# Statistics matmuls in four column tiles, the last score level in two halves of the array, a new order of the opening and five smaller edits in a hybrid RG-LRU / HGRN2 / SSD layer

## The chip, the cores and the metric

The kernel runs on one core of a Trainium2 chip. The metric is the device time of one execution in microseconds (us), the median of three runs. A profiled execution stands beside it: its trace gives the start and the length of each instruction on each engine. PE is the matrix engine (PEld its weight loads), DVE the vector engine, ACT the scalar engine, POOL the GpSimd engine, and SP the queue that issues most of the transfers from memory.

## The reference, cut to what matters

One decoder layer on 2048 tokens of width 1024; three mixers share one input projection (1024 to 5648 columns) and one output projection (2048 to 1024).

```python
h = rmsnorm(x, norm_w) * (1 + scale) + shift        # scale, shift = cond @ w_ada
u = h @ w_in                                        # split over the three mixers
ya = rg_lru(conv(a_x), ...) * silu(a_g)             # 512 wide
yb = rmsnorm(hgrn2_chunked(q, k, v, log_f), hg_norm_w) * silu(hg_g)   # 512 wide, 4 heads
yc = groupwise rmsnorm(ssd_chunked(...) * silu(ssd_z))                # 1024 wide, 2 groups
y = concat([ya, yb, yc]) @ w_out
out = rmsnorm(x + gate * y)
```

All matrix work is in float32. The projections split each operand into a rounded high and a low part (float32r) and run three passes, high by high, high by low and low by high; the small matmuls take plain float32 operands, and the trace shows two records for each of those.

## The kernel before, in words

The tokens are handled in four blocks of 512, two at a time: a first half (blocks 0 and 1) and a second half (blocks 2 and 3). Channels lie on the partitions, tokens along the free axis.

*The opening.* For the first two blocks the string `PROG` (line 41) writes out the order of the opening by hand, one token for each step. `X` loads a block of transposed x (eight transfers of 256 KB), `D` loads one of eight pieces of the modulation weights (four transfers of 256 KB, line 434), `w` and `W` load and split the first three projection weights, in two halves of the contraction. `S` squares x on ACT and sums the squares on DVE (`norm_sum`, line 299; seven additions), `Q` sums over the partitions on PE (line 311), `R` spreads the result over the partitions (line 320, evacuated by ACT). `A` is the modulation matmul of one piece (line 441, 16 records in the trace), whose result ACT copies to `macc`; `C` turns it into a column (line 450) that DVE finishes. `H` with block and piece makes one piece of h: DVE scales x (`h_pre`), ACT writes the high part (line 330), DVE the low part (line 332). `M` with block and piece are the nine matmuls of that piece for the forget, query and gate projections of head 0 (line 339). `U` is a number of warming matmuls on ones (line 1004). PE runs its instructions in exactly this order; a scheduler places those of the other engines. SP issues transfers in order and keeps eight of them under way.

*The rest of a half.* `weave` (line 382) spreads the serial work of a branch between the pieces of the next projections: a branch is a generator, each of its `yield`s has a weight, and after each the share of the pieces that is due is written. `pend` is the list of branches for the next stretch of projections.

- `hgrn` (line 553) is the gated recurrence of one head for both blocks: seven score levels (levels 0 to 5 in column tiles of 32, `ps_sA` and `ps_sB`; the last, `ps_sC`, line 609, with 64 weight columns), between them multiplications of Q and K on DVE and POOL; then transposes (`ps_kt`), the state products (`ps_kv`), and the output `ps_o` (lines 645 and 649), block after block in the single bank of the pool `ps_oy`.
- `stats` (line 521) sums the squares of a branch's outputs, `acc`, over the channels: four matmuls for a block, the weights 128 tokens of `acc`, the moving operand one column of ones. There are two for each of the three norms in each half.
- `ssd_bc`, `ssd_a`, `ssd_b` are the state space branch; its `ps_y` (lines 792 and 797) writes the two halves of the partitions in turn, 64 weight columns each. `lru` is the RG-LRU, whose activations are chained in order by `sact` (line 151).
- `norm_gen` (line 883) makes the norm of blocks 2 and 3 during the first half: square root on ACT, reciprocal on DVE (line 285), `ps_rb` on PE.

*The output projection.* `fetch` (line 913) reads a group's branch outputs back and splits them, the low part by default on POOL, and `unit` runs the matmuls `po` (line 1138).

## Time and profile before

| what | us |
|---|---|
| median of 3 runs (1697.58 to 1697.99) | 1697.59 |
| the profiled execution, its own time | 1699.3 |
| its span, from the first instruction to the last | 1697.5 |
| PE busy with matmuls | 1653.0 (97%) |
| DVE / ACT / POOL busy | 971.5 / 748.6 / 757.3 |

The times that follow are counted from the start of the span. A group of instructions carries its line, its engine, and output<-inputs by the names in the program; a bracket behind it gives the idle time of its engine just before and what ended that. Matmuls are pipelined: how long a block of them holds PE is read from its start to the start of the next block, not from the length of one.

### The profile page before, as it was taken

Reading aid. Unit: us, or ns where it says so; the run is one execution under the profiler, and the core shown is the slowest. Engines: PE = TensorE matmul, PEld = TensorE weight load, DVE = VectorE, ACT = ScalarE, POOL = GpSimd, SP = SyncE. Lnnn points to the kernel's source line nnn. Section 1 sums busy time; section 2 is a strip of 40 time slices with the busy share of each in tenths; the row PEclk is TensorE's granted clock in tenths of the full one; section 3 lists DMA queues with packets and bytes.
Section 4 is the critical chain, followed back from the end, with each engine's and each line's share of the span. In section 5 each row is a group of like instructions: output and inputs, shape, how many; then the busy total and the mean of one; then the engine's idle time right before and its main releaser. Section 6 shows DMA issues by size and latency. Waiting matters only on the chain.

```text
span 1697.5 us, 29336 instructions
## 1 busy us (share of the span) xinstructions
PE 1653.0 (97%) x11452; PEld 1349.2 (79%) x11452; DVE 971.5 (57%) x1726; ACT 748.6 (44%) x1640; POOL 757.3 (45%) x630
## 2 busy tenths in 40 slices
PE   8799999999999999899999999999999999999998
PEld 4688877888887877788887788888877777888886
DVE  5654766557645746646756555655568646444443
ACT  4422323366556656632322456554757623222221
POOL 1233344355635764345334346545756543222223
PEclk9899999999999999999999999999999999999999
DMA  9412010032425342231110032323334544333231
GB/s 333 116 26 63 27 39 26 26 113 82 116 71 155 88 125 76 62 89 45 29 55 27 27 100 75 94 56 106 88 103 133 171 120 150 97 96 99 89 93 61
DMA packets 177691, 150.60 MB, mean 89 GB/s; under 512 B 14545, under 2 KB 137937, under 8 KB 177553
## 3 DMA queue, kind: packets, MB, share of 16 engines
q1 hardware_dynamic: 141216, 123.82, 25.1%
q10 hardware_dynamic: 33936, 17.04, 3.4%
q0 software_dynamic: 2400, 7.87, 1.3%
q8 instruction: 90, 1.47, 0.4%
q14 instruction: 49, 0.39, 0.1%
HBM read 123.40 MB, written 25.30 MB: 88 GB/s over the span
## 4 chain that ended last, share of the span: by engine, by line
PE 85%; DVE 4%; DMA 3%; ACT 3%; issue 3%; POOL 2%; SPq 0%; POOLq 0%; ACTq 0%; DVEq 0%
PE po L1138 19%; PE ps_x L339 10%; PE ps_z L339 9%; PE ps_v L345 6%; PE ps_f L339 5%; PE ps_g L339 5%; PE ps_bc L339 5%; PE ps_q L339 4%; PE ps_lg L339 4%; PE ps_lx L339 4%; PE ps_y L792 2%; PE ps_bx L768 2%; PE ps_y L797 1%; PE ps_sA L565 1%; PE ps_o L645 1%
## 5 line engine op out<-in xcount | busy, mean ns | idle before, releaser
L1138 PE MATMUL po<-wo,yy 128*128 128x512 f32 x1512 | 353.3, 395 | 2.5 <-POOL yy L69 1.6
L1138 PEld LDWEIGHTS po<-wo,yy 128*128 128x128 f32 x1512 | 283.8, 188 | 71.5 <-POOL yy L69 2.4
L142 POOL TENSOR_TENSOR w<-raw,w 128x512 fp32r<-128x512 f32 x156 | 219.6, 1426 | 266.9 <-ACT w L141 223.4
L72 DVE SCALAR_TENSOR_TENSOR cacc<-craw,col,cacc 128x512 f32<-128x512 f32 x192 | 203.8, 1062 | 47.6 <-ACT cacc L66 36.3
L339 PE MATMUL ps_z<-ht,w 128*128 128x512 f32 x768 | 190.2, 399 | 0.8 <-ACT halo L66 0.8
L339 PE MATMUL ps_x<-ht,w 128*128 128x512 f32 x768 | 190.4, 400 | 0.0
L339 PEld LDWEIGHTS ps_z<-ht,w 128*128 128x128 f32 x768 | 141.9, 188 | 34.7 <-issue 2.1
L339 PEld LDWEIGHTS ps_x<-ht,w 128*128 128x128 f32 x768 | 141.1, 189 | 28.6
L72 DVE SCALAR_TENSOR_TENSOR o<-po,rstd,o 128x512 f32<-128x512 f32 x64 | 47.2, 749 | 119.4 <-PE po L1138 98.8
L69 POOL TENSOR_TENSOR yy<-yr,yy 128x512 fp32r<-128x512 f32 x61 | 78.7, 1310 | 80.7 <-ACT yy L66 73.4
L69 POOL TENSOR_TENSOR hg_k<-hg_k,hg_t 128x256 f32<-128x256 f32 x80 | 60.2, 770 | 120.6 <-PE ps_sA L565 61.3
L141 ACT ACTIVATE w<-raw 128x512 fp32r<-128x512 f32 x158 | 92.3, 627 | 42.0 <-issue 22.0
L339 PE MATMUL ps_f<-ht,w 128*128 128x512 f32 x384 | 99.5, 406 | 5.4 <-DVE ht L72 5.4
L339 PE MATMUL ps_bc<-ht,w 128*128 128x512 f32 x384 | 101.0, 406 | 0.0
L345 PE MATMUL ps_v<-vw,ht 128*128 128x264 f32 x768 | 98.8, 289 | 0.0
L339 PE MATMUL ps_q<-ht,w 128*128 128x512 f32 x384 | 98.7, 403 | 0.0
L339 PE MATMUL ps_lx<-ht,w 128*128 128x512 f32 x384 | 97.7, 408 | 0.0
L345 PEld LDWEIGHTS ps_v<-vw,ht 128*128 128x128 f32 x768 | 95.7, 191 | 1.2 <-DVE l_gs L69 0.2
L69 POOL TENSOR_TENSOR s_ce<-s_ce,cacc 128x512 f32<-128x512 f32 x64 | 93.5, 1481 | 1.5 <-ACT s_ce L66 1.5
L339 PE MATMUL ps_lg<-ht,w 128*128 128x512 f32 x384 | 93.2, 397 | 0.0
L339 PE MATMUL ps_g<-ht,w 128*128 128x512 f32 x336 | 92.0, 408 | 0.0
L339 PEld LDWEIGHTS ps_f<-ht,w 128*128 128x128 f32 x384 | 71.2, 191 | 23.4 <-DVE ht L72 5.7
(260 smaller groups left out, 2853.1 us busy)
## 6 DMA issues: line engine op xcount, KB each, us to landing
raw<-in_w_in SPq DMA_DIRECT2D x176, 256.0 KB, 3.2
s_cb<-crd SPq DMA_DIRECT2D x64, 256.0 KB, 3.8
yr<-yscr SPq DMA_DIRECT2D x64, 256.0 KB, 3.2
xr<-in_x SPq DMA_DIRECT2D x48, 256.0 KB, 3.4
xt<-in_x_t SPq DMA_DIRECT2D x32, 256.0 KB, 4.7
wta<-in_w_mod SPq DMA_DIRECT2D x32, 256.0 KB, 5.9
yscr<-cacc ACTq DMA_DIRECT2D x32, 256.0 KB, 2.7
rawo<-in_w_out SPq DMA_DIRECT2D x32, 256.0 KB, 3.9
```

Of the source, the lines that this page charges most:

```text
L69: e.tensor_tensor(o, a, b, op=op)
L72: V.scalar_tensor_tensor(o, a, s, b, op0=op0, op1=op1)
L141: after(S.activation(hi, raw, AF.Copy), None if eng is V else dep)
L142: after(eng.tensor_tensor(lo, raw, hi, op=SUB), dep if eng is V else None)
L339: d_ = PE.matmul(ps, b.hl[wl][:, k, :], ht[:, hl, :], start=(k == 0 and n == 0), stop=(k == KT - 1 and n == 2))
L345: d_ = PE.matmul(ps[:, 0:264], ht[:, hl, c * P:(c + 1) * P], b.vw[k // 4][wl][:, k % 4, :], start=(k == 0 and n == 0), stop=(k == KT - 1 a ...
L565: PE.matmul(out(n, c, r), Ks[n][:, o:o + 32], mv[n][..., o + sh:o + sh + 32], start=True, stop=True)
L645: PE.matmul(po[:, c], v[:, c], ssb[:, 4 * n + c], start=True, stop=ci == 0)
L768: PE.matmul(pkv[:, c].rearrange("p h n -> p (h n)"), bt[:, c], xw[:, c].rearrange("p h n -> p (h n)"), start=True, stop=True)
L792: PE.matmul(py[64 * hh:64 * hh + 64, c], xdt[:, c, hh], Ms[hh][:, c], start=True, stop=sv[tb][c] is None)
L797: PE.matmul(py[64 * hh:64 * hh + 64, c], sv[tb][c][:, 64 * hh:64 * hh + 64], Cs[hh][:, c * P:(c + 1) * P], start=False, stop=True)
L1138: PE.matmul(pss[t, n], yys[u, t][yl][:, k4, :], wts[4 * fam + k4][wl][n], start=(k4 == 0 and i == 0), stop=(k4 == 3 and i == 2))
```

## The change

1. `PROG` is written anew. The second block of x is loaded behind the third modulation piece instead of ahead of the eighth, its squares and its norm come before M03, and from then on the pieces of both blocks alternate. The squares of both blocks share four buffers of the weight pool, and the first x takes buffers of the pool for h. Two warming matmuls are added before M03. Each scaling (`h_pre`) is ordered behind the low part of the piece before the last.
2. The 32 row parameters (`rowp`) are loaded at the start by ACT's queue, and `aneg` is made from them there, not at the end of the first half's recurrences.
3. `stats` takes both blocks in one go; each group of 128 tokens becomes four matmuls with 32 weight columns, in four column tiles: 32 matmuls instead of 2 x 4.
4. The last score level puts the first block on partitions 0 to 63 and the second on 64 to 127, and alternates between them; two copies evacuate it.
5. `ps_o` of the second block takes a bank of `ps_sc`.
6. Each `hgrn` gets a gap of weight 2 ahead of it.
7. Square root and reciprocal of the norms of blocks 2 and 3 are made ahead of the second RG-LRU stretch, both at once.
8. The low part of units 4 and 5 of the output projection is made by DVE.

```diff
-PROG = ("X0 D0 w0 D1 D2 S0 U8 A0 Q0 U1 C0 D3 R0 W0 A1 U1 C1 H00 D4 A2 M00 C2 H01 w1 W1 D5 A3 M01 C3 H02 D6 A4 M02 C4 H03 X1 "
-        "A5 M03 C5 H04 D7 A6 M04 C6 H05 S1 M05 H06 Q1 A7 R1 M06 C7 H10 H07 B K M10 H11 M11 H12 M07 H13 M12 H14 M13 "
-        "H15 M14 H16 M15 H17 E M16 M17")
+PROG = ("X0 D0 w0 D1 D2 X1 S0 U8 A0 Q0 U1 C0 D3 R0 W0 A1 U1 C1 H00 H01 A2 M00 C2 w1 H02 M01 S1 M02 D4 A3 Q1 C3 R1 H03 "
+        "H10 U2 W1 M03 D5 A4 M10 H11 C4 M11 H12 H04 M12 H13 M13 D6 A5 M04 H14 C5 H05 M14 D7 A6 M05 H15 C6 H06 M15 A7 M06 H16 C7 "
+        "H07 B K M16 H17 E M07 M17")
...
-        after(nc.sync.dma_start(rowp, rows[0:1, 0:32].to_broadcast([P, 32])), dep)
...
     def early():
+        nc.scalar.dma_start(rowp, rows[0:1, 0:32].to_broadcast([P, 32]))
...
+        sact(aneg, rowp[:, 16:32], AF.Exp)
+        V.tensor_scalar(aneg, aneg, -1.0, None, op0=MUL)
...
-    def stats(acc, fam, tb):
+    def stats(accs, fam, tbs):
         yield
         pq = bank(ps_ms, "ms", "pq")
-        for i in range(4):
-            PE.matmul(pq[:, i:i + 1], acc[:, i * P:(i + 1) * P], ones[:, 0:1], start=True, stop=True)
-        act(ssq[:, fam, 4 * tb:4 * tb + 4], pq[:, 0:4], AF.Copy)
+        for n, tb in enumerate(tbs):
+            for i in range(4):
+                for r in range(4):
+                    o = i * P + 32 * r
+                    PE.matmul(pq[32 * r:32 * r + 32, 4 * n + i:4 * n + i + 1], accs[tb][:, o:o + 32], ones[:, 0:1],
+                              start=True, stop=True)
+        act(ssq[:, fam, 4 * tbs[0]:4 * tbs[0] + 8], pq[:, 0:8], AF.Copy)
         yield
...
+                for c in range(4):
+                    for n in range(2):
+                        o = c * P
+                        PE.matmul(pC[64 * n:64 * n + 64, c], Ks[n][:, o:o + 64], Qs[n][:, o + 64:o + P],
+                                  start=True, stop=True)
                 for n in range(2):
-                    for c in range(4):
-                        o = c * P
-                        PE.matmul(pC[0:64, 4 * n + c], Ks[n][:, o:o + 64], Qs[n][:, o + 64:o + P],
-                                  start=True, stop=True)
-                act(ssb[0:64, :, 64:P], pC[0:64], AF.Copy)
+                    act(ssb[0:64, 4 * n:4 * n + 4, 64:P], pC[64 * n:64 * n + 64, 0:4], AF.Copy)
...
-            po = bank(ps_oy, "oy", "ps_o", (P, 4, P))
+            pool, tag = ((ps_oy, "oy"), (ps_sc, "sc"))[n]
+            po = bank(pool, tag, "ps_o", (P, 4, P))
...
     def norm_gen(xs, st):
-        rb = norm_rows(rsqrt_cols(st))
+        rb = norm_rows(st)
...
-                sqs = [[hp.tile([P, 2, TB], F32, tag="h", name="xsq") for _ in range(4)] for _ in tbs]
-                x0s = [wp.tile([P, 2, TB], F32, tag="w", name="xt") for _ in range(4)]
+                x0s = [hp.tile([P, 2, TB], F32, tag="h", name="xt") for _ in range(4)]
+                sqs = [wp.tile([P, 2, TB], F32, tag="w", name="xsq") for _ in range(4)]
...
-            pend = [(hgrn(h, tbs, {tb: fq[h, tb] for tb in tbs}, {tb: vs[tb][0] for tb in tbs}, acc, h == 0), HGW)]
+            pend = [(gap(2), 2), (hgrn(h, tbs, {tb: fq[h, tb] for tb in tbs}, {tb: vs[tb][0] for tb in tbs}, acc, h == 0), HGW)]
...
-        if half == 0:
-            act(aneg, rowp[:, 16:32], AF.Exp)
-            V.tensor_scalar(aneg, aneg, -1.0, None, op0=MUL)
...
-        st_ = [(stats(acc[tb], 0, tb), 2) for tb in tbs]
+        st_ = [(stats(acc, 0, tbs), 2)]
...
-            late = [(stats(acc[tb], 1 + g, tb), 2) for tb in tbs]
+            late = [(stats(acc, 1 + g, tbs), 2)]
...
+            if i == 1 and half == 0:
+                xst = {n: rsqrt_cols(st) for n, st in xst.items()}
...
-            fetch(u + 1)
+            fetch(u + 1, V if u + 1 in (4, 5) else G)
```

Three places show where the instructions went.

ACT in the opening. `xt_210` and `xt_211` before, and `xt_205` and `xt_206` in the change, are buffers of the first block's x, `xt_255` to `xt_269` in the change the pieces of the second block's; `ht` is the high part of a piece of h. Before:

```order
L66 ACTIVATE rb_320<-ps_rb_315 128x512
L141 ACTIVATE wt_326<-raw_238 128x512
L330 ACTIVATE ht_350<-xt_210,gsc_83 128x512
L66 ACTIVATE macc_339<-psm_330 128x256
L330 ACTIVATE ht_388<-xt_210,gsc_83 128x512
L66 ACTIVATE macc_370<-psm_361 128x256
```

In the change:

```order
L66 ACTIVATE xsq_209<-xt_255 128x512
L330 ACTIVATE ht_365<-xt_205,gsc_83 128x512
L66 ACTIVATE xsq_209<-xt_257 128x512
L66 ACTIVATE macc_354<-psm_345 128x256
L66 ACTIVATE xsq_210<-xt_259 128x512
L66 ACTIVATE xsq_210<-xt_261 128x512
L66 ACTIVATE xsq_211<-xt_263 128x512
L66 ACTIVATE xsq_211<-xt_265 128x512
L66 ACTIVATE macc_381<-psm_372 128x256
L66 ACTIVATE xsq_212<-xt_267 128x512
L330 ACTIVATE ht_369<-xt_205,gsc_83 128x512
```

The squares of the second block now stand ahead of the first two pieces of h and of the copies of the second and third modulation results; before, they stood behind all but two of the first block's pieces.

PE at the end of the first half's third stretch of projections (`ps_bc`), around the statistics of the recurrence. Before:

```order
L649 MATMUL ps_o<-hg_q,hst_177 128x128
L339 MATMUL ps_bc<-ht,w 128x512 x3
L525 MATMUL pq<-ones,acc 128x1 x4
L339 MATMUL ps_bc<-ht,w 128x512 x6
L525 MATMUL pq<-ones,acc 128x1 x4
L669 MATMUL ps_bt<-ident,cacc 128x128 x4
```

In the change:

```order
L653 MATMUL ps_o<-ssb,hg_v 128x128
L657 MATMUL ps_o<-hg_q,hst_180 128x128
L339 MATMUL ps_bc<-ht,w 128x512 x6
L530 MATMUL pq<-ones,acc 32x1 x32
L677 MATMUL ps_bt<-ident,cacc 128x128 x4
```

The sums of the second block stood nine projection matmuls behind the last output, and now stand six behind it.

ACT around the square root of the norm of block 3 (`xst_5300` before, `xst_5347` in the change; `xst_5044` is that of block 2). Before, at the start of the second half:

```order
L152 ACTIVATE l_r_6806<-ps_r_6802,col_74 128x512
L152 ACTIVATE l_i_6808<-ps_i_6803,col_74 128x512
L152 ACT_TABLE_LOAD
L152 ACTIVATE xst_5300<-xst_5300,epsc_92 128x4
L141 ACTIVATE w_6734<-raw_6736 128x512
L141 ACTIVATE w_6734<-raw_6740 128x512
L66 ACTIVATE rb_6825<-ps_rb_6820 128x512
```

In the change, ahead of the activations of the first RG-LRU stretch:

```order
L152 ACTIVATE l_gs_6185<-ps_lg_6118 128x512
L152 ACT_TABLE_LOAD
L152 ACTIVATE xst_5044<-xst_5044,epsc_92 128x4
L152 ACTIVATE xst_5347<-xst_5347,epsc_92 128x4
L66 ACTIVATE s_z_5910<-cacc_5783 128x512
L520 DMA yscr1_100<-cacc_5783 128x4x128
L152 ACT_TABLE_LOAD
L152 ACTIVATE l_r_6206<-ps_r_6202,col_74 128x512
```

Both roots now come some eighty microseconds of PE work earlier, with one more table load on either side of them.

## Rows read from the trace of the kernel before

**Rows 1.** The page's first two parts: the span, and the busy time of each engine.

```profile
span 1697.5 us, 29336 instructions
...
PE 1653.0 (97%) x11452; PEld 1349.2 (79%) x11452; DVE 971.5 (57%) x1726; ACT 748.6 (44%) x1640; POOL 757.3 (45%) x630
```

**Rows 2.** Who waited for whom on PE, over the whole span: the line that waited, what it waited for, us in total, times, the longest.

```profile
PE ps_rb L320 <- DVE xst L285: 7.3, 2, 5.5
PE ps_f L339 <- DVE ht L72: 5.4, 1, 5.4
PE ps_ss L311 <- DVE xsq L305: 3.9, 1, 3.9
PE psm L450 <- ACT macc L66: 2.9, 1, 2.9
...
PE ps_o L645 <- DVE hg_g L69: 1.9, 2, 1.1
PE ps_sA L565 <- POOL hg_q L69: 1.8, 1, 1.8
PE po L1138 <- POOL yy L69: 1.6, 2, 0.9
```

**Rows 3.** PE in order of time, in the opening (start, length, instructions with their count, idle time before them in brackets).

```profile
21.40 1.86 PE L441 MATMUL psm<-wta,condz 128*32 128x256 f32 x16
...
37.37 0.50 PE L450 MATMUL psm<-ones,macc 128*128 128x1 f32 x4
37.80 1.07 PE L441 MATMUL psm<-wta,condz 128*32 128x256 f32 x16
...
71.18 0.86 PE L339 MATMUL ps_f<-ht,w 128*128 128x512 f32 x3
...
73.26 0.86 PE L339 MATMUL ps_f<-ht,w 128*128 128x512 f32 x3
...
85.10 0.86 PE L339 MATMUL ps_g<-ht,wt 128*128 128x512 f32 x3
...
88.36 0.65 PE L565 MATMUL ps_sA<-hg_q,hg_k 128*32 128x64 f32 x32 [1.82 <-POOL hg_q L69]
```

**Rows 4.** Windows of the opening and of the start of the second half: length, busy time of PE, PEld, DVE, ACT and POOL with counts, then PE's granted clock, the share of the transfer engines and GB/s.

```profile
65.00:70.00 5.00, 5.00 (x12) 3.91 (x13) 4.84 (x7) 4.17 (x7) 2.58 (x2) 0.51 0.03 10
693.00:698.00 5.00, 4.99 (x23) 4.99 (x24) 2.24 (x2) 2.99 (x6) 3.98 (x4) 0.50 0.47 134
```

**Rows 5.** SP's queue of transfers in the opening, in order of time: start and length of the issuing.

```profile
11.12 11.82 SPq L434 DMA_DIRECT2D wta<-in_w_mod  x16
...
31.85 5.01 SPq L279 DMA_DIRECT2D xt<-in_x_t  x8
```

**Rows 6.** Time from issue to landing of the modulation weights (the tile wta) up to 60 us.

```profile
DMA to landing us min/median/max: 5.1/5.9/6.6
```

**Rows 7.** ACT in order of time, in the opening.

```profile
19.46 0.72 ACT L330 ACTIVATE ht<-xt,gsc 128x512 fp32r<-128x512 f32 x1 [0.30 <-DVE xt L72]
20.13 0.38 ACT L66 ACTIVATE macc<-psm 128x256 f32<-128x256 f32 x1
...
43.54 4.26 ACT L66 ACTIVATE xsq<-xt 128x512 f32<-128x512 f32 x8
```

**Rows 8.** DVE in order of time, in the opening.

```profile
20.22 0.75 DVE L72 SCALAR_TENSOR_TENSOR ht<-xt,gsc,ht 128x512 fp32r<-128x512 f32 x1 [0.19 <-ACT ht L330]
...
44.71 0.69 DVE L305 TENSOR_TENSOR xsq<-xsq 128x512 f32<-128x512 f32 x1 [0.29 <-ACT xsq L66]
```

**Rows 9.** PE in order of time around a block of statistics, the last score level, and a score level of 64 records in four column tiles.

```profile
108.33 0.76 PE L565 MATMUL ps_sB<-hg_q,hg_k 128*32 128x32 f32 x64
109.03 1.23 PE L345 MATMUL ps_v<-vw,ht 128*128 128x264 f32 x8
...
127.86 1.15 PE L609 MATMUL ps_sC<-hg_q,hg_k 128*64 128x64 f32 x16
128.94 2.35 PE L339 MATMUL ps_q<-ht,w 128*128 128x512 f32 x9
...
314.06 0.95 PE L525 MATMUL pq<-ones,acc 128*128 128x1 f32 x8
314.87 1.66 PE L339 MATMUL ps_bc<-ht,w 128*128 128x512 f32 x6
```

**Rows 10.** PE groups by line, shape and tile: count, busy us, mean ns of one, idle time before.

```profile
L525 PE MATMUL pq<-ones,acc 128*128 128x1 f32 x96 | 11.4, 239 | 0.0
...
L609 PE MATMUL ps_sC<-hg_q,hg_k 128*64 128x64 f32 x128 | 9.6, 225 | 2.3 <-DVE hg_q L69 2.3
```

**Rows 11.** PE in order of time where `ps_y` alternates between the two halves of the array.

```profile
597.35 0.39 PE L792 MATMUL ps_y<-s_cb,s_xdt 128*64 128x128 f32 x4
...
599.53 0.39 PE L792 MATMUL ps_y<-s_cb,s_xdt 128*64 128x128 f32 x4
```

**Rows 12.** The end of the recurrence at 313 us: ACT's square of the second block, and POOL's addition to acc.

```profile
313.62 0.60 ACT L66 ACTIVATE hg_f<-ps_o 128x512 f32<-128x512 f32 x1 [4.07 <-PE ps_o L649]
...
314.30 1.28 POOL L69 TENSOR_TENSOR acc<-acc,hg_f 128x512 f32<-128x512 f32 x1 [4.29 <-ACT hg_f L66]
```

**Rows 13.** ACT and DVE at the start of the second half.

```profile
692.29 0.30 ACT L152 ACTIVATE xst<-xst,epsc 128x4 f32<-128x4 f32 x1
...
692.79 0.17 DVE L285 RECIPROCAL xst<-xst 128x4 f32<-128x4 f32 x1
```

More of the change, by code (lines that the diff above doesn't have):

```diff
@@ L323, in norm_rows, with h_pre @@
         return rb
-    def h_pre(xs, rb, k):
-        stt(xs[k], xs[k], gsc[:, 1, k:k + 1], rb, MUL, MUL)
+    def h_pre(xs, rb, k, dep=None):
+        after(V.scalar_tensor_tensor(xs[k], xs[k], gsc[:, 1, k:k + 1], rb, op0=MUL, op1=MUL), dep)
     def h_tile(xs, k, dep=None):
@@ L893, in some, with gap @@
             yield w_
-    def gap():
-        yield
+    def gap(w=1):
+        yield w
     def h_build(tb, xs, hts, dep):
@@ L1044, in trunk @@
             run(ps_, pend)
-            pend = [(hgrn(h, tbs, {tb: fq[h, tb] for tb in tbs}, {tb: vs[tb][1] for tb in tbs}, acc, False), HGW)]
-        if half == 0:
-            act(aneg, rowp[:, 16:32], AF.Exp)
-            V.tensor_scalar(aneg, aneg, -1.0, None, op0=MUL)
+            pend = [(gap(2), 2), (hgrn(h, tbs, {tb: fq[h, tb] for tb in tbs}, {tb: vs[tb][1] for tb in tbs}, acc, False), HGW)]
         dt_ = [(ssd_dt(tb, dtr[tb], dts), 1) for tb in tbs]
-        st_ = [(stats(acc[tb], 0, tb), 2) for tb in tbs]
+        st_ = [(stats(acc, 0, tbs), 2)]
         pend = dt_ + pend + st_
```

12 lines of the change are left out of this document (7 added, 5 removed).

## Prediction

> **What bounds the kernel now.** The page's first part shows PE busy for 1653.0 of 1697.5 us, every other engine below 60% [rows 1]. So a microsecond counts only if it is PE work or PE idle time. Next I read PE's waits [rows 2]: DVE's `xst` holds `ps_rb` for 7.3 us in two waits, the longest 5.5; the opening holds three single waits of 5.4, 3.9 and 2.9 us; then come 1.9 for `ps_o`, 1.8 for the first `ps_sA`, 1.6 for POOL's `yy`. PE in order of time tells the unit prices of the opening [rows 3]: a piece M costs 2.08 us warm (71.18 to 73.26, nine matmuls), a modulation A 1.07 warm and 1.86 cold, a column C 0.43, and the last M ends at 85.96. The clock [rows 4] is at 0.51 in the 5 us behind the wait of 5.4 and at 0.50 in the 5 us behind the one of 5.5, which is the 1.2 GHz level: each wait costs 2.5 us more.
>
> **The change, part by part.** *Opening.* SP issues the 16 modulation quarters in 11.82 us, 0.74 each [rows 5], and one lands 5.9 us after its issue [rows 6]. The second x now stands behind the eighth of them, so its first piece is issued at 11.12 + 8.5 x 0.74 = 17.4 and lands at 23.3. The change's order puts the first square ahead of the first high part on ACT, and the second ahead of the copy of A1. A square takes 4.26 / 8 = 0.53 [rows 7]; pieces land 0.74 apart, so the second is squared by 24.0 + 0.53 = 24.6 and the copy (0.38 [rows 7]) ends near 25.1, where that copy began at 20.13 before. PE reaches C1 near 21.7 and stands idle for some 4 us: this is a **new wait**, and A2 and M00 are queued behind it. With a cold A2 and M00, M00 ends near 30.5. DVE has seven additions of 0.69 for the squares [rows 8] between its scalings and low parts (0.75 each [rows 8]), so the low part of H01 comes at 30.9, M01 ends at 33.0, the low part of H02 comes at 34.9 and M02 ends at 37.1. Then A3 (1.07), Q1 and R1 (0.9, an estimate at the price of two C), the copy (0.38), C3 (0.43), DVE's finish (0.4, an estimate at the price of the copy), scaling, high part and low part (0.75, 0.72 [rows 7], 0.75) lead to M03 at 42.4, which ends at 44.5. From there both blocks have their pieces ready by turns: twelve M, four A and four C are 25.0 + 4.3 + 1.7 = 31.0 us, and with 1.5 for short waits M17 ends at 77, against 85.96: **-8.9**. Bounds: nothing gained (first rival) and -14.7, all three opening waits gone (12.2) with one cold stretch (2.5). I take the chain's value, since each of its steps has a row. The eight pieces of x, before issued at 31.85 [rows 5], no longer hold back weights there, while D4 to D7 are issued later; the last, D7, lands by some 50 at the same 0.74 and 5.9 and is wanted at 66 by the count of M, A and C, so they cost nothing, and a late one would cost at most about the 5.4 already seen. U2 adds under 1 us inside the wait for M03: nothing.
>
> *First `ps_sA`.* Before it, 24 `ps_v` matmuls now cover POOL's `hg_q` (eight take 1.23 [rows 9]; three times that is above 1.82 [rows 3]): **-1.8**.
>
> *`ps_rb`.* Roots (0.30) and reciprocals (0.17 [rows 13]) are made a stretch ahead, so both waits go, **-7.3**, and the cold 5 us with them, **-2.5**. What is late next is a free bank, or the activations that the two extra table loads push back by about 3 us, with banks full of finished matmuls ahead of PE; taken as nothing, upper bound the wait of 5.5 that they remove, with its cold 2.5.
>
> *Statistics.* Eight records of `pq` hold PE from 314.06 to 314.87, 0.81 us [rows 9]; the 96 records [rows 10] are 12 such blocks, 9.7. They become six blocks of 64 records (32 matmuls, two records each). The nearest row is `ps_sB`: 64 records in four column tiles, 0.70 us from start to start [rows 9], plus 0.1 for entering: 0.79 x 6 = 4.7, so **-5.0**. Bounds: +5.3, if each record keeps a quarter of today's 0.81 / 8 = 0.101 us (64 x 0.039 = 2.5 a block, 15.0 in all), and -5.5 with no entry. I take `ps_sB`, since count, tiles and output rows are the same and only the moving operand is narrower (1 column instead of 32).
> The Trainium skill, in "TensorEngine Tiling (Array Packing)", section "Performance Considerations", speaks against this part: each matmul carries a fixed overhead of about 60 cycles, so a dimension that is already small should not be cut further. At 2.4 GHz that page's figure gives an estimate of 25 ns a record, 64 records 1.6 us, and the term would be zero. By that page this trace disagrees: its 64 narrow records take 0.70 us, 11 ns each.
> The sum now waits for both blocks. At 313.62 ACT squares the second output (0.60) and POOL adds it until 315.58 [rows 12], some 2.4 us after the last `ps_o`; six projection matmuls (1.4) stand between, so a wait of 0.5 to 1 is left in each half: **+1.0**, bounds 0 and two of 2.4.
>
> *Last score level.* 16 records take 1.08 us [rows 9], in 8 places (128 records in all [rows 10]). Where `ps_y` alternates halves of the array, a row of four takes 0.218 (ten rows from 597.35 to 599.53 [rows 11]), 54.5 ns a record of 128 columns. Half of `ps_sC`'s 1.08 should go under the other half, less some entry: 0.46 each, **-3.7**; bounds 0 and -4.3. The second evacuating copy adds some 0.2 us to ACT, which is 44% busy: nothing.
>
> *Second bank for `ps_o`*: its waits go, **-1.9** [rows 2]. *Low part on DVE*: POOL's `yy` goes, **-1.6** [rows 2]; DVE is at 57% [rows 1]. `aneg` and `rowp` move to an ACT that waits for the first transfers; the gap only shifts the recurrences among projections: nothing each, at worst one more wait of the 1.9 kind.
>
> Sum: -8.9 - 1.8 - 7.3 - 2.5 - 5.0 + 1.0 - 3.7 - 1.9 - 1.6 = -31.7. The profiled execution took 1699.3 us, 1667.6 after it; the median of the runs lay 1.7 below it, so 1665.9, **1666**.
>
> **The rivals.** *First, the opening gains nothing.* The new wait for the squares grows: any lateness of the second x goes straight onto C1, and every weight piece behind it on SP is later too. Against it stands that the three old waits have no cause left. Without -8.9 and -1.8: 1677.
> *Second, the wait of `ps_rb` comes back as one for a bank or for ACT.* For it: two more table loads in a chained order of activations; against: the roots depend on nothing from that stretch. Without -7.3 and -2.5: 1676.
> *Third, the tiles of the statistics do not pay.* Records that each write a single column might not follow at 11 ns. At 0.101 / 4 = 25 ns the term is gone: 1671. At 39 ns it is +5.3: 1676.
> *Fourth, waits only move.* Of the waits, all come back elsewhere, and PE work alone is saved: -5.0 - 3.7, with the +1.0: 1697.6 - 7.7 = 1690; some of it within 0.2% if the score level does not overlap either.
> *Fifth, on the other side: the opening stays cold.* The new wait near 21.7 and many short ones after it could keep PE at 1.2 GHz from there to M17, where before it fell only behind single waits. At 0.51 [rows 4] an M costs 2.08 / 0.51 = 4.1, which is 2.0 more, and a cold A 0.8 more than a warm one [rows 3]: 16 M and 7 A make 37.6 us more PE work. It decides from 31.6 of that on the path (1697.6 - 1666); all of it gives 1704. The windows speak against it: PE was back at full pace some 5 us after each wait.
>
> **How the numbers follow.** A measurement of this kernel can tell about 0.2% (3.4 us) from no change. Forecast 0.58, by itself 1659 to 1672; opening 0.14; `ps_rb` 0.12; tiles 0.08; moved waits 0.04; cold opening 0.04. The range 1657 to 1679 takes in the forecast with its bounds and the first three rivals singly, and leaves out the last two and two rivals together. Faster: all but the fifth and half of the fourth, 0.94; same 0.02; slower 0.04.
>
> **What would show it.** Right: PE idle some 4 us near 22 with `psm` behind ACT's `macc`, none above 2 us after 45, M17 ending near 77; `ps_rb` with no wait for `xst` and a granted clock near 1 at the start of the second half; `pq` blocks of 64 records moving on in 0.8 us; `ps_sC` in 0.6; no `yy` among POOL's releases. Wrong: M17 beyond 83, `pq` above 1.6 us a block, or a single new wait above 4 us past the opening.

## The result: 0.9856 of the time before, and the profile after

The change takes 1674.5 us (median of 4 runs, 1673.66 to 1675.43), beside 1697.79 for the kernel before (four runs, 1697.58 to 1702.84): a ratio of 0.9856, 95% interval 0.9837 to 0.9875, 23.3 us faster. The forecast was 1666, with a range of 1657 to 1679. The sign and the range held; 8.5 us of the forecast gain did not come.

The profiled execution's own time is 1674.89 us, its span 1672.4 against 1697.5 [rows 1]. The page's span and its busy times:

```profile
span 1672.4 us, 29921 instructions
...
PE 1641.3 (98%) x11744; PEld 1335.6 (80%) x11744; DVE 965.2 (58%) x1728; ACT 748.6 (45%) x1641; POOL 755.9 (45%) x628
```

PE has 11.7 us less work than in [rows 1], and the span is shorter by 25.1, so a little over half of the gain is idle time. PE's waits by what it waited for (line that waited, what for, us in total, times, the longest), the counterpart of [rows 2]:

```profile
PE psm L450 <- ACT macc L66: 3.7, 1, 3.7
PE ps_f L339 <- DVE ht L332: 2.2, 4, 1.0
PE ps_f L339 <- ACT ht L330: 1.7, 3, 0.9
PE ps_sC L615 <- DVE hg_q L69: 1.6, 2, 0.8
...
PE ps_sB L571 <- DVE hg_q L69: 1.0, 2, 0.5
...
PE ps_kv L643 <- ACT hg_kt L66: 0.9, 2, 0.5
PE po L1147 <- POOL yy L69: 0.9, 2, 0.5
```

Of the rows that carried the sum, `xst`, `xsq` and `hg_g` are gone, as is the first `ps_sA` behind POOL; what the forecast had called new, `psm` behind ACT's `macc`, leads the list with 3.7 us. Four small kinds stand there that no term had: `ps_f` behind `ht` (seven waits), `ps_sB`, `ps_kv` and a larger `ps_r` (1.0); further down the list `ps_f` waits 0.7 once for the copy of dt.

Where the 25.1 us come from can be read from PE's starts alone. Each line of this table is the time from one first matmul to the next, worked out from the starts of those matmuls in the two traces:

| stage (first matmul to first matmul) | before | change | difference |
|---|---|---|---|
| start to `ps_v` | 88.95 | 81.06 | -7.89 |
| to `ps_bc` (recurrences) | 185.81 | 185.02 | -0.79 |
| to `ps_x` | 42.81 | 40.94 | -1.87 |
| to `ps_lx` (state space branch) | 257.17 | 255.45 | -1.72 |
| to `ps_v` of the second half | 111.47 | 108.48 | -2.99 |
| to its `ps_bc` | 233.06 | 225.43 | -7.63 |
| to its `ps_x` | 42.80 | 41.88 | -0.92 |
| to its `ps_lx` | 255.32 | 254.25 | -1.07 |
| to the end | 480.14 | 479.95 | -0.19 |

In the change the first score level stands behind 24 `ps_v` matmuls, so 1.15 us of its work has moved from the first stage to the second; the opening's own gain is 85.96 - 81.06 = 4.9.

PE in the opening (start, length, instructions, in brackets the idle time before them and what ended it), the counterpart of [rows 3]:

```profile
24.92 1.01 PE L450 MATMUL psm<-ones,macc 128*128 128x1 f32 x4 [3.73 <-ACT macc L66]
...
42.90 1.26 PE L339 MATMUL ps_f<-ht,w 128*128 128x512 f32 x3
...
55.14 0.73 PE L339 MATMUL ps_f<-ht,w 128*128 128x512 f32 x2 [1.00 <-DVE ht L332]
...
75.28 0.50 PE L339 MATMUL ps_f<-ht,w 128*128 128x512 f32 x1 [0.57 <-ACT ht L330]
76.06 0.74 PE L339 MATMUL ps_f<-ht,w 128*128 128x512 f32 x2 [0.28 <-DVE ht L332]
...
79.09 0.73 PE L339 MATMUL ps_f<-ht,w 128*128 128x512 f32 x2 [0.66 <-DVE ht L332]
...
81.06 3.06 PE L345 MATMUL ps_v<-vw,ht 128*128 128x264 f32 x24
```

The first line is C1, the second M03; the waits at 55.14, at 75.28 and 76.06, and at 79.09 belong to M13, M07 and M17, and the last line stands where M17 ends. C1 waits 3.73 us where the chain had put some 4, M03 starts at 42.90 where it had 42.4: the first half of the chain is right to within 1.0 us at each step. From the end of M03 at 45.5 to the last M it takes 35.6 us and not 32.5.

The granted clock, as [rows 4] (same columns): the stretch behind the new wait and the start of the second half.

```profile
26.00:31.00 5.00, 5.00 (x24) 3.05 (x23) 4.18 (x9) 2.98 (x6) 0.00 (x0) 0.50 1.09 361
676.00:692.00 16.00, 15.18 (x97) 13.53 (x96) 16.00 (x17) 10.23 (x27) 8.10 (x5) 1.00 0.40 112
```

The second half now starts at full clock. A2 and M00 ran at the 1.2 GHz level behind C1's wait, which the chain had priced.

The statistics and the last score level, PE in order of time, as [rows 9], and their groups (lower fence, the columns of [rows 10]):

```profile
122.61 0.69 PE L615 MATMUL ps_sC<-hg_q,hg_k 128*64 128x64 f32 x16
123.22 0.96 PE L339 MATMUL ps_q<-ht,w 128*128 128x512 f32 x3
...
287.40 0.33 PE L615 MATMUL ps_sC<-hg_q,hg_k 128*64 128x64 f32 x2
288.53 0.65 PE L615 MATMUL ps_sC<-hg_q,hg_k 128*64 128x64 f32 x14 [0.80 <-DVE hg_q L69]
289.11 2.36 PE L339 MATMUL ps_bc<-ht,w 128*128 128x512 f32 x9
...
305.44 0.43 PE L530 MATMUL pq<-ones,acc 128*32 128x1 f32 x32
306.24 0.43 PE L530 MATMUL pq<-ones,acc 128*32 128x1 f32 x32 [0.37 <-POOL acc L69]
306.60 0.66 PE L677 MATMUL ps_bt<-ident,cacc 128*128 128x128 f32 x4
```

```profile
L615 PE MATMUL ps_sC<-hg_q,hg_k 128*64 128x64 f32 x128 | 7.0, 230 | 3.0 <-DVE hg_q L69 1.6 <-POOL hg_k L69 1.0 <-DVE hg_t L69 0.4
...
L530 PE MATMUL pq<-ones,acc 128*32 128x1 f32 x384 | 4.6, 172 | 0.7 <-POOL acc L69 0.7
```

The 64 records of a block go from 305.44 to 306.60, less the wait of 0.37: 0.79 us, the forecast's price to the hundredth. The four blocks that do not wait hold PE 0.64 us each, from start to start, and the projection matmul ahead of each 0.1 longer.

The last score level shrank from 9.6 us of busy time to 7.0, not by 3.7. In three of its eight places it does not wait, and there 16 records hold PE 0.61 us (122.61 to 123.22) where [rows 9] had 1.08: the forecast's 0.46 is saved. In the other five an operand comes late, and the new order lets only two records run ahead of that wait, since the third already belongs to the second block (287.40 and 288.53); without the wait such a place still holds PE 0.91 to 0.94 us. Before, the whole first block stood ahead of the second block's wait:

```profile
295.32 0.65 PE L609 MATMUL ps_sC<-hg_q,hg_k 128*64 128x64 f32 x8 [0.21 <-DVE hg_q L69]
296.73 0.65 PE L609 MATMUL ps_sC<-hg_q,hg_k 128*64 128x64 f32 x8 [0.76 <-DVE hg_q L69]
```

### The profile page after: what moved, and what is told of

Read it like the earlier page. It is cut to its first block, busy times and chain, and to the rows that moved or that the text cites. A ratio compares the mean times of both kernels' runs of the same rounds, so it can differ in the third digit from the quotient of the medians.

```text
span 1672.4 us, 29921 instructions
## 1 busy us (share of the span) xinstructions
PE 1641.3 (98%) x11744; PEld 1335.6 (80%) x11744; DVE 965.2 (58%) x1728; ACT 748.6 (45%) x1641; POOL 755.9 (45%) x628
## 4 chain that ended last, share of the span: by engine, by line
PE 85%; DVE 5%; ACT 3%; issue 2%; DMA 2%; POOL 2%; SPq 0%; ACTq 0%; POOLq 0%; DVEq 0%
PE po L1147 20%; PE ps_x L339 10%; PE ps_z L339 10%; PE ps_f L339 5%; PE ps_g L339 5%; PE ps_v L345 5%; PE ps_lx L339 4%; PE ps_bc L339 4%; PE ps_lg L339 4%; PE ps_q L339 3%; PE ps_y L800 2%; PE ps_bx L776 2%; PE ps_y L805 1%; DVE hg_q L69 1%; DVE cacc L72 1%
```

## The experiments

Times are given as ratios to the kernel before, run beside each on the same chip, since the median of the kernel before lay between 1697.8 and 1700.3 us from one set of runs to the next; 0.001 is 1.7 us. The intervals are 0.0013 to 0.0023 to either side, and a difference from the change has the interval of both; so what is smaller than some 4 us is read from the spans, and from the stages of single profiled executions. The brackets behind a span give the lowest and highest of all executions of that kernel.

| kernel | ratio | 95% interval | span | first `ps_v` |
|---|---|---|---|---|
| the change | 0.9856 | 0.9837 to 0.9875 | 1672.4 (1671.6 to 1672.4) | 81.06 |
| u_open | 0.9883 | 0.9868 to 0.9898 | 1678.7 (1676.4 to 1678.8) | 85.91 |
| u_stats | 0.9870 | 0.9855 to 0.9885 | 1676.7 (1675.4 to 1676.7) | 81.04 |
| u_score | 0.9892 | 0.9870 to 0.9915 | 1678.2 (1677.8 to 1683.8) | 81.16 |
| u_roots | 0.9903 | 0.9886 to 0.9920 | 1682.0 (1681.0 to 1682.3) | 81.44 |
| u_gap | 0.9852 | 0.9837 to 0.9866 | 1672.9 (1672.9 to 1673.7) | 84.51 |
| u_bank | 0.9901 | 0.9888 to 0.9915 | 1682.1 (1680.4 to 1682.1) | 81.08 |
| u_yy | 0.9863 | 0.9850 to 0.9877 | 1674.5 (1673.5 to 1677.1) | 81.55 |
| w1_early | 0.9859 | 0.9842 to 0.9875 | 1671.1 (1671.1 to 1675.2) | 78.88 |
| w1_dve | 0.9847 | 0.9834 to 0.9861 | 1671.5 (1671.5 to 1672.8) | 78.45 |
| b_early | 0.9856 | 0.9841 to 0.9871 | 1673.6 (1672.0 to 1675.5) | 81.08 |
| x1_late | 0.9826 | 0.9812 to 0.9841 | 1668.4 (1666.9 to 1670.9) | 75.74 |
| x1_masks | 0.9825 | 0.9812 to 0.9838 | 1666.9 (1666.9 to 1669.3) | 74.35 |

Two ratios alone, those of u_roots and u_bank, have intervals clear of the change's. The first `ps_v` starts where the last M ends, save in u_gap, where the first score level stands between (its last M ends at 80.5).

M03 begins at 41.6 to 43.4 us in the nine traces whose order is the same up to it, since the clock behind C1's wait comes back sooner in some (granted clock 0.50 to 0.72 over 26 to 31 us). From M03 to the first `ps_v`, the change and the five kernels that leave this stretch alone and start `ps_v` behind it take 38.12 to 38.16 us. So what an edit behind M03 gains in the opening is read from M03 on.

### One part of the change taken back

**u_open**, the old opening (its buffers go back too, not shown):

```diff
-PROG = ("X0 D0 w0 D1 D2 X1 S0 U8 A0 Q0 U1 C0 D3 R0 W0 A1 ...")
+PROG = ("X0 D0 w0 D1 D2 S0 U8 A0 Q0 U1 C0 D3 R0 W0 A1 ...")      # the string of the kernel before
-                        h_pre(xsb[ar[0]], sts[ar[0]], ar[1], los[-2])
+                        h_pre(xsb[ar[0]], sts[ar[0]], ar[1])
```

> The change with the old order of the opening alone put back (its buffers and the free order of the scalings too); the gap ahead of the recurrences stays. Theory from the two traces: the new opening gained 4.9 us at its end (last M 85.96 before, 81.06 in the change), and the first score level's wait of 1.8 is covered by the gap and not by the opening, so the median is 1674.5 + 4.9 = 1679.4, the last M of the opening ends at 86. Rival: the forecast's 8.9 was there and something else lost it, so 1683.4. Second rival: waits only move, later transfers catch up, 1674.5 within 1.

The last M ends at 85.9, 4.85 later, and the ratio rises by 0.0027 (4.6 us). The span grows by 6.3: the further 1.4 lies behind the opening, 1.1 of it in the recurrences of the second half, where the wait of `ps_f` for the copy of dt is 1.70 instead of 0.70. No wait of `ps_sA` for POOL is left in this kernel, so the gap covers it and not the opening. The first theory holds: the opening was worth 4.9, not the forecast's 8.9.

**u_roots**, the roots late again:

```diff
-            if i == 1 and half == 0:
-                xst = {n: rsqrt_cols(st) for n, st in xst.items()}
-        rb = norm_rows(st)
+        rb = norm_rows(rsqrt_cols(st))
```

> The change with roots and reciprocals of the norms of blocks 2 and 3 made late again, each where its norm is used. Theory: both waits of ps_rb (7.3) and the 5 us at half clock (2.5) come back, +9.8, less the new waits of 0.8 at ps_r and 0.7 at the dt copy that the early roots brought: +8.3, 1682.8, granted clock near 0.5 for 5 us at the start of the second half. Rival: the clock's share is not regained, +7.3, 1681.8. Second rival: the waits come back with other neighbours and are covered now by other projections, under +3.

The span grows by 9.6, the ratio by 0.0047 (8.0 us). PE (first fence) waits again, and the granted clock of the five microseconds behind it (second fence, the columns of [rows 4]) falls to 0.74:

```profile
635.36 1.16 PE L320 MATMUL ps_rb<-ident,xst 128*128 128x128 f32 x8 [1.73 <-DVE xst L285]
...
680.75 2.08 PE L320 MATMUL ps_rb<-ident,xst 128*128 128x128 f32 x8 [5.62 <-DVE xst L285]
```

```profile
681.00:686.00 5.00, 5.00 (x32) 5.00 (x33) 2.50 (x3) 3.20 (x9) 4.17 (x4) 0.74 0.41 113
```

Both waits are back in full (7.3 in all), the clock costs 5 x 0.26 = 1.3 where [rows 4] had 2.5, and the two stages with the waits grow by 2.0 and 5.9; the other 1.7 of the span lies in stages without any of them (0.4 in the opening, 0.8 in the output projection). So the roots were worth some 8 us, the largest term of the gain, as the first theory has it; the clock is back at 1.00 some 3 us after the wait (684 to 686 us), where before it stayed at 0.50 for 5.

**u_stats**, the statistics matmuls wide again:

```diff
-                for r in range(4):
-                    o = i * P + 32 * r
-                    PE.matmul(pq[32 * r:32 * r + 32, ...], accs[tb][:, o:o + 32], ones[:, 0:1], ...)
+                o = i * P
+                PE.matmul(pq[:, 4 * n + i:4 * n + i + 1], accs[tb][:, o:o + P], ones[:, 0:1], ...)
```

> The change with the statistics matmuls 128 tokens wide again (16 records for both blocks together instead of 64 in four column tiles); both blocks still together. Theory: a block of 16 records holds PE 1.6 us against 0.78 for the 64 narrow ones, six times, so +5.0: 1679.5. Rival: the narrow tiles pay nothing (25 ns a record), so 1674.5 within 1. Second rival: the wait for acc ahead of the block shrinks as the block grows, +4.

The span grows by 4.3, the ratio by 0.0014 (2.4 us, with an interval that takes in the 4.3). In the trace a block of 16 records goes from 305.30 to 307.10, 1.80 us, with no wait for acc, where the change has 0.79 and a wait of 0.37 (the blocks that do not wait in the change: 1.70 instead of 0.64); the six stages in which the blocks lie grew by 0.48, 1.24, 0.93, 0.51, 0.88 and 0.22. The second rival is nearest: the first block's records cover the wait for acc when they are wide, so that the narrow ones give 0.7 of their gain back.

**u_score**, the old last score level:

```diff
-                for c in range(4):
-                    for n in range(2):
+                for n in range(2):
+                    for c in range(4):
                         o = c * P
-                        PE.matmul(pC[64 * n:64 * n + 64, c], Ks[n][:, o:o + 64], Qs[n][:, o + 64:o + P], ...)
+                        PE.matmul(pC[0:64, 4 * n + c], Ks[n][:, o:o + 64], Qs[n][:, o + 64:o + P], ...)
-                for n in range(2):
-                    act(ssb[0:64, 4 * n:4 * n + 4, 64:P], pC[64 * n:64 * n + 64, 0:4], AF.Copy)
+                act(ssb[0:64, :, 64:P], pC[0:64], AF.Copy)
```

> The change with the old last score level (both blocks on partitions 0 to 63, one after the other, one copy). Theory from the groups: 128 records are busy 9.6 us before and 7.0 in the change, +2.6: 1677.1. Rival, the forecast's price: +3.7, 1678.2. Second rival: PE waits for DVE or POOL at this place anyway, so 1674.5 within 1.

The ratio rises by 0.0036 (6.1 us), the span by 5.8, more than any of the three. The stages of the recurrences, four of the table's nine, grow by 3.9. The matmuls give 2.9 of it (9.9 us busy against 7.0), with shorter waits of `ps_sC` and `ps_kv`, but there is a wait that neither the change nor the kernel before has: ACT (first fence) and PE (second) at the end of the second recurrence.

```profile
293.22 0.63 ACT L66 ACTIVATE craw<-cacc 128x512 f32<-128x512 f32 x1 [5.07 <-DVE cacc L72]
293.88 0.59 ACT L66 ACTIVATE ssb<-ps_sC 64x512 f32<-64x512 f32 x1
```

```profile
294.61 0.63 PE L633 MATMUL ps_kt<-ident,hg_k 128*128 128x128 f32 x4 [1.71 <-ACT ssb L66]
```

The single copy of `ps_sC` stands on ACT behind a copy to `craw` that waits for DVE until 293.22, and the transposes of the second block wait 1.71 us for it (1.99 in the second half). In the change its two copies ran at once behind the matmuls, and in the kernel before the one copy did too, at 297.41, ahead of that `craw`. So the 3.9 is the price of this part in this order of ACT, not the part's gain over the kernel before, which the groups put at 2.6. Another 1.8 of the span is a wait of `ps_z` for ACT's halo at 526 us, 2.06 where the change has 0.27; in the other traces it lies between 0.47 and 1.57, and whether it belongs to this edit stays open.

**u_gap**, no gap ahead of the recurrences (taken out at both places, one shown):

```diff
-            pend = [(gap(2), 2), (hgrn(h, tbs, ..., h == 0), HGW)]
+            pend = [(hgrn(h, tbs, ..., h == 0), HGW)]
```

> The change without the gap of weight 2 ahead of each recurrence. Theory: the first score level stands again right behind the opening and waits for POOL's query (1.8 us), nothing covers it: 1676.3. The other recurrences move by a few projection matmuls; their waits for DVE and POOL (sB 1.5, sC 3.0, kv 0.9 in the change; sC 2.3, kt 0.8, sA 1.2 before) change by under 1: in all 1675.5 to 1677. Rival: the gap is what brought the new waits for sB and kv, and without it they go, 1674.5.

Both were right in mechanism, and they cancel. POOL's query holds the first score level again:

```profile
81.26 0.65 PE L571 MATMUL ps_sA<-hg_q,hg_k 128*32 128x64 f32 x32 [0.80 <-POOL hg_q L69]
83.80 0.78 PE L571 MATMUL ps_sA<-hg_q,hg_k 128*32 128x64 f32 x32 [1.89 <-POOL hg_q L69]
```

That is 2.7 us back in the opening. But the waits of `ps_sC` fall from 3.0 to 0.8 and its 16 records hold PE 0.61 us in five of the eight places, the waits of `ps_sB` and `ps_kv` for DVE and ACT go, and `ps_kt` waits 1.42 twice in their place: the four stages of the recurrences become 2.6 us shorter (with the first score level's 1.15 set to the same stage). The span is 0.5 longer, the ratio 0.0004 lower. The gap's term of -1.8 was right where it was put, and was paid back in the recurrences.

**u_bank**, `ps_o` in one bank:

```diff
-            pool, tag = ((ps_oy, "oy"), (ps_sc, "sc"))[n]
+            pool, tag = (ps_oy, "oy")
             po = bank(pool, tag, "ps_o", (P, 4, P))
```

> The change with ps_o of both blocks in the one bank of ps_oy again. Theory, the forecast's term: the two waits of about 1 us for DVE's gate come back at the end of the second and fourth recurrence, +1.9: span 1674.3. Rival: the gap ahead of the recurrences has moved the outputs to where other projections cover them, under 0.5: span 1672.4 within 0.5.

Neither: the ratio rises by 0.0045 (7.6 us), the span by 9.7. PE's waits:

```profile
PE ps_o L653 <- DVE hg_g L69: 5.4, 5, 1.5
...
PE ps_f L339 <- ACT dtr L66: 1.8, 1, 1.8
```

In the kernel before the same bank cost two waits and 1.9 us; here it costs five and 5.4, and a wait for the copy of dt that is 1.1 longer, behind which the clock is at 0.93 over 676 to 692 us where it is 1.00 in the change. So the second bank is worth far more in the changed kernel than its wait before showed. What made the single bank dearer was not separated: the gap, which sets the outputs to other places among the projections, is the likeliest of the other edits, but no run had both taken back.

**u_yy**, the low parts of units 4 and 5 on POOL:

```diff
-            fetch(u + 1, V if u + 1 in (4, 5) else G)
+            fetch(u + 1)
```

> The change with the low parts of units 4 and 5 of the output projection made by POOL again. Theory: POOL's yy held PE 1.6 us in two waits before and holds it 0.9 in two others in the change, so +0.7: span 1673.1. Rival, the forecast's term: +1.6, span 1674.0. Second rival: the waits only move to the next units, 1672.4 within 0.3.

The ratio rises by 0.0007, inside its interval; the span by 2.1. The waits for `yy` are 0.49 and 0.97 in place of 0.39 and 0.47, so 0.6 of it is this edit by the trace; 0.5 came from an opening that began slower, and the rest stays open. The forecast's 1.6 was too much: `yy` of the first such unit holds PE in the change as well.

### Where the opening lost its 4 us

In the change DVE is slow just where M13 is late. DVE in order of time (first fence) and POOL (second):

```profile
44.64 0.75 DVE L332 SCALAR_TENSOR_TENSOR ht<-xt,gsc,ht 128x512 fp32r<-128x512 f32 x1
45.31 1.79 DVE L326 SCALAR_TENSOR_TENSOR xt<-xt,gsc,rb 128x512 f32<-128x512 f32 x1
47.02 3.48 DVE L332 SCALAR_TENSOR_TENSOR ht<-xt,gsc,ht 128x512 fp32r<-128x512 f32 x2
```

```profile
45.21 3.05 POOL L142 TENSOR_TENSOR w<-raw,w 128x512 fp32r<-128x512 f32 x2 [42.27 <-ACT w L141]
48.21 1.75 POOL L142 TENSOR_TENSOR wt<-raw,wt 128x512 fp32r<-128x512 f32 x1
```

A scaling or low part of 0.75 takes 1.77 to 1.79 while POOL makes the low parts of the weights, three of them (not the four that two expectations below count), and POOL's take 1.75 where 1.29 is usual. Three runs test this, and two more try the opening's other losses. The expectations of b_early and x1_masks call two pieces M16 and M07 that are M07 and M17 by the order of `PROG`; behind the expectations they have their own names.

**w1_early**, the split one step earlier:

```diff
-        ... w1 H02 M01 S1 M02 D4 A3 Q1 C3 R1 H03 H10 U2 W1 M03 ...
+        ... w1 H02 M01 S1 W1 M02 D4 A3 Q1 C3 R1 H03 H10 U2 M03 ...
```

> The change with the second half of the first projection weights split one step earlier (before M02 instead of before M03), so that POOL's three low parts fall into a stretch where DVE is idle. Theory: in the change DVE's scalings and low parts take 1.78 us instead of 0.75 while POOL works on those parts (45.2 to 50.0), four of them, which makes the low part of H13 late and costs PE 1.6 us at 53.3 to 55.1; that goes, and the last M ends at 79.5: 1672.9. Rival: the lateness comes from the order rule of the scalings, and stays: 1674.5 within 0.5. The other side: the splits now hold ACT and DVE ahead of the low part of H03, and M03 comes up to 2 later, 1676.5.

POOL (first fence) now works while DVE is idle, and DVE (second) has its usual durations at the place where it was slow:

```profile
35.18 2.58 POOL L142 TENSOR_TENSOR w<-raw,w 128x512 fp32r<-128x512 f32 x2 [32.24 <-ACT w L141]
37.73 1.29 POOL L142 TENSOR_TENSOR wt<-raw,wt 128x512 fp32r<-128x512 f32 x1
```

```profile
44.16 0.75 DVE L332 SCALAR_TENSOR_TENSOR ht<-xt,gsc,ht 128x512 fp32r<-128x512 f32 x1
44.83 0.74 DVE L326 SCALAR_TENSOR_TENSOR xt<-xt,gsc,rb 128x512 f32<-128x512 f32 x1
45.50 1.62 DVE L332 SCALAR_TENSOR_TENSOR ht<-xt,gsc,ht 128x512 fp32r<-128x512 f32 x2
```

The idle time ahead of M13 is gone and the last M ends at 78.9, 2.2 earlier: 0.5 of it by M03, and 1.7 from M03 on (36.46 us for 38.16), where the theory had 1.6. The theory holds for the opening. The time does not show it: the profiled span is 1.3 shorter, but the other three are 1673.9 to 1675.2, above the change's, and the ratio is the same.

**w1_dve**, the same low parts on DVE:

```diff
-                            b_.parts(ar[0], *((dn, V) if ar[0] == 0 else (hn, G)))
+                            b_.parts(ar[0], *((dn, V) if ar[0] == 0 else (hn, V)))
```

> The change with the low parts of the second half of the first projection weights made by DVE instead of POOL, at the same place in the program. Theory: what cost PE 1.6 us ahead of M13 is POOL's activity, which stretches each of DVE's operations from 0.75 to 1.78; with POOL idle DVE has three operations of 0.69 more (2.1 us) but four shorter by 1.03 (4.1 us), so no operation of 1.7 us is left between 43 and 51 and the wait shrinks to under 0.5: 1673.3. Rival: it is the number of operations ahead of the low part of H13, and DVE with three more of them is later still, wait above 2, 1676. Second rival: it is ACT's splits, nothing changes, 1674.5.

DVE has three operations more, and is done earlier:

```profile
43.15 1.29 DVE L142 TENSOR_TENSOR w<-raw,w 128x512 fp32r<-128x512 f32 x2
44.35 0.69 DVE L142 TENSOR_TENSOR wt<-raw,wt 128x512 fp32r<-128x512 f32 x1
44.95 0.75 DVE L332 SCALAR_TENSOR_TENSOR ht<-xt,gsc,ht 128x512 fp32r<-128x512 f32 x1
...
46.28 1.63 DVE L332 SCALAR_TENSOR_TENSOR ht<-xt,gsc,ht 128x512 fp32r<-128x512 f32 x2
```

No wait of PE for DVE over 0.3 us stands between 34 and 72 us; the last M ends at 78.45, 2.6 earlier. Half of this, 1.3, is there by M03, up to which PE's program is the same (granted clock 0.72 instead of 0.50 over 26 to 31 us); the other 1.3 comes behind it, with M13's wait gone and M10 0.3 slower. The number of operations ahead (first rival) and ACT's splits, which remain (second rival), are both excluded: POOL's activity makes M13 late. A gain in the time is not shown: the ratio falls by 0.0009, inside its interval, and the four spans are those of the change. In the profiled execution a wait of `ps_z` at 520 us was 1.57, and 0.27 in that of the change.

**b_early**, the value weights two pieces earlier:

```diff
-        ... H05 M14 D7 A6 ... H07 B K M16 H17 E M07 M17
+        ... H05 M14 D7 B A6 ... H07 K M16 H17 E M07 M17
```

> The change with the first value weights split two pieces earlier (behind M14 instead of behind M06), so that POOL's low parts of them fall at 58 to 64 and no longer at 71 to 78. Theory: DVE's slow operations at 72.7 to 79.0 (0.88, 1.27, 1.78 us where 0.16, 0.15 and 0.75 are usual) go, and with them the waits of 1.5 and 1.0 us ahead of M16 and M07; some come back at 61 to 64 where DVE has 2.5 us of slack: 1672.5. Rival: DVE is slowed there in the same way and PE waits for that instead: 1674.5 within 0.7.

The rival was right. The slow place moves along with POOL: DVE (first fence), POOL (second) and PE (third).

```profile
67.56 3.44 DVE L326 SCALAR_TENSOR_TENSOR xt<-xt,gsc,rb 128x512 f32<-128x512 f32 x2
```

```profile
66.22 4.23 POOL L142 TENSOR_TENSOR vw<-raw,vw 128x512 fp32r<-128x512 f32 x3
```

```profile
71.71 0.74 PE L339 MATMUL ps_f<-ht,w 128*128 128x512 f32 x2 [0.96 <-DVE ht L332]
```

Two scalings take 3.44 us there and PE waits 0.96 for what follows, at M06. M17 no longer waits, M07 still does for 0.28, and the last M ends at 81.1 as in the change; from M03 on 0.4 is gained, which M03 had begun later.

**x1_late**, the second x behind D3:

```diff
-PROG = ("X0 D0 w0 D1 D2 X1 S0 U8 A0 Q0 U1 C0 D3 R0 ...
+PROG = ("X0 D0 w0 D1 D2 S0 U8 A0 Q0 U1 C0 D3 X1 R0 ...
```

> The change with the second block of x loaded behind D3 instead of behind D2, which puts the copies of the first modulation results ahead of its squares on ACT. Theory: the wait of C1 for macc (3.7 us at 24.9) goes, A2 and M00 start 4 us earlier, the squares are ready in time for Q1 and M03 starts at 39 instead of 42.9: last M ends at 77, 1670.5. Rival: x comes four transfers (2.9 us) later, its sum is late for Q1, and M03 starts no earlier: 1674.5, with idle PE in front of ps_ss in place of C1's. The other side: 1676 if the second block's pieces stay late to the end.

The copy of A1 comes at 20.43 on ACT and C1 runs with no wait; M03 begins 3.9 us earlier, and the last M ends at 75.74, 5.3 earlier:

```profile
21.28 0.50 PE L450 MATMUL psm<-ones,macc 128*128 128x1 f32 x4
...
33.66 1.05 PE L311 MATMUL ps_ss<-ones,xsq 128*128 128x1 f32 x8 [0.67 <-DVE xsq L305]
...
39.04 1.51 PE L339 MATMUL ps_f<-ht,w 128*128 128x512 f32 x3
```

The rival's idle time in front of `ps_ss` is there, with 0.67 us. The ratio is 0.0030 below the change's (5 us), the span 4.0, and all four spans lie below all of the change's: the theory holds, and the new wait that the forecast named was the price of loading x that early. Of the 5.3, 3.9 is there by M03. The rest comes behind it: M13 does not wait here, although DVE is as slow beside POOL (1.77 to 1.79 at 40.0 to 45.2), since the granted clock of 0.66 over 36 to 41 us holds up PE ahead of M03 and DVE gains on it.

**x1_masks**, the same with the masks behind the last low part:

```diff
-        "H07 B K M16 H17 E M07 M17")
+        "H07 B M16 H17 E K M07 M17")
-        V.tensor_copy(maskd, mf[:, 0])
+        after(V.tensor_copy(maskd, mf[:, 0]), lo)       # lo: the last low part of h
```

> The second x behind D3, as in x1_late, and besides DVE's two copies of the masks behind the last low part of h instead of ahead of it (1.27 us there, stretched by POOL). Theory: x1_late's gain of 3.4 to 4.0 stays, and the wait ahead of M07 (0.67 idle, 1.0 from start to start) goes: span 1667.4, the time 0.0005 of the ratio below x1_late's, the best of all. Rival: the low part itself is stretched by POOL in its new place, and the wait stays: 1668.4 as x1_late.

M17 no longer waits, M07 still does (0.58 and 0.28), and the last M ends at 74.35. Of these 1.4 us, 1.0 comes back as a longer wait of the first score level for POOL (0.93). The 1.4 is not the edit's alone: M03 began 1.9 earlier in this execution, without x1_late's slow stretch ahead of it, and the wait ahead of M13 (1.00 at 49.33) is there again. The ratio equals x1_late's: theory in the mechanism, rival in the time. Both kernels are faster than the change by all their spans and their first `ps_v`; the intervals of their ratios touch its lower end.

## Why the prediction was right, and what was mis-sized

| term | forecast | measured | by |
|---|---|---|---|
| opening | -8.9 | -4.9 | last M; u_open |
| first `ps_sA` | -1.8 | its waits are gone; 2.6 paid back later | u_gap |
| `ps_rb` and clock | -9.8 | -8 to -9.6 | ratio and span of u_roots |
| statistics with their wait | -4.0 | -4.4; span of u_stats -4.3 | groups, waits |
| last score level | -3.7 | -2.6, and 0.7 more waiting; -0.46 a place where nothing waits | groups, waits, starts |
| `ps_o` | -1.9 | its waits are gone | waits; u_bank |
| POOL's `yy` | -1.6 | -0.6 to -0.7 | u_yy; waits |

The time came out inside the range, but outside the forecast's own 1659 to 1672: the opening gave about half of its term, which is half of the first rival. That the range held is owed to the rivals in it.

*Right:* that PE's work and idle time are the only ones that count; the two roots with the clock behind them; the narrow matmuls at 0.79 a block, taken from the row with the same count and tiles; the wait for acc, 0.7 for a forecast 1.0; C1's wait, 3.7 for some 4, and its cause, which x1_late takes away.

*The step that failed* is "From there both blocks have their pieces ready by turns", with its "1.5 for short waits". The short waits came to 3.9: against the usual spacing of starts PE loses 1.6 us at M13 (53.3 to 55.7 for its first three matmuls, where 0.7 is usual), 1.4 at M07 (74.5 to 76.6) and 0.9 at M17 (78.0 to 79.7). DVE's scalings and low parts were priced at 0.75 throughout. Three of them take 1.77 to 1.79 beside POOL's low parts of the weights at 45 to 50 us, and w1_early and w1_dve show that this is what makes M13 late. Between 72 and 79 us, beside POOL's low parts of the value weights, a small addition for C7 takes 0.88 (0.16 alone), the copy of the masks 1.27 (0.15 before) and a low part 1.77. Moving the copy frees M17 (x1_masks), and moving POOL's work moves the wait (b_early); how much of M07's 1.4 is POOL's no run shows. A second thing was missing: an M behind an A or a C takes 2.2 instead of 2.08 (the first three matmuls move on in 0.79, the others in 0.70), which is about 1 over the eight pieces that follow one. The last 1.0 lies ahead: M03 ended at 45.5 for 44.5. Against these stand some 0.5 by which A and C moved on faster than priced (1.00 and 0.36). Had I laid POOL's order beside DVE's as I did ACT's, the first would have been on the page: the kernel before has such rows too, but there the long DVE stretches stood beside larger waits.

The Trainium skill states a rule that bears on this, in "SBUF — State Buffer", section "Who interferes with whom": a DVE instruction with two inputs in SBUF and a GpSimd instruction that reads SBUF exclude each other for a whole instruction, and whichever comes second waits. This case's trace agrees: POOL's first low part runs from 45.21, DVE's scaling begins at 45.31 and takes 1.79, and from then on the two take turns, one DVE operation every 1.7 us and one POOL operation every 1.7 us, where a DVE operation alone takes 0.75 and a POOL one 1.29. The two are not shut out for quite their whole length: a pair takes 1.71, and alone they move on in 0.67 and 1.25, together 1.92.

*Smaller misses.* The score level gave 2.6 for 3.7. Half of its records did hide under the other half, at the forecast's price, in the three places without a wait and in five of eight in u_gap; the forecast had not asked whether the second block's operands are there. By turns, the records of the first block stand behind the second block's wait, and in the changed kernel, with the gap, that wait comes more often (3.0 us for 2.3). The recurrences got new waits for `ps_sB` and `ps_kv`, 2.3 us in all, with the gap (u_gap); `ps_r` behind ACT grew by 0.8, `po` behind DVE's `l_gs` by 0.5, and the copy of dt holds PE 0.7. These 4.3 were the fourth rival's kind, at under a fifth of its size (1690 for 1666). Last, the forecast took the median to lie 1.7 below the profiled execution, as before; it lies 0.4 below it here, which alone is 1.3 of the 8.5.

*The account:* the opening lacks 4.0, the later stages 2.7 (forecast -21.0, measured -18.3 from the table of stages, with the first score level's 1.15 set to where it was), the time outside the span 0.7 and the median 1.3, in all 8.7 for a difference of 8.5 (1674.5 - 1666).

*The third rival* did not come to pass: at 0.79 us for 64 records these take 12 ns each, not 25, and u_stats gives the gain. The Trainium skill's fixed overhead of about 60 cycles a matmul ("TensorEngine Tiling (Array Packing)", section "Performance Considerations") was counted for a record, and so counted this case's traces do not show it for matmuls in four column tiles. Counted for a matmul of the program, of two records each, they show 0.64 to 0.79 us for 32, 20 to 25 ns, which is near the 25 ns that the prediction estimated from the page; the page does not say which it means.

The parts do not add up one by one: the spans of the seven kernels with one part taken back grow by 6.3, 4.3, 5.8, 9.6, 0.5, 9.7 and 2.1, in all 38, for 25.1 of the whole. A part taken back from the finished kernel shows what it is worth there (the bank, the score level's two copies), not what it added to the kernel before. Two parts have no run of their own: the early row parameters and the two warming matmuls ahead of M03.

## What to carry to other kernels

Where a chain runs over DVE, lay POOL's order beside it before pricing it: two operations that are cheap alone took turns and more than doubled DVE's price here. An input that is loaded early also puts its first use early on the engine that handles it, ahead of what the critical chain needs there; look for the latest place at which it is still in time. A small matmul is priced best from a row with the same number of records and the same tiles. And where two blocks' matmuls are made to alternate, ask first when the second block's operands come: from its first record on, both blocks wait for them.
